# Gated delta recurrence: keys' norms through ScalarE's Ln and Exp, one PSUM reader in the convolution, and the first latent columns handed out ahead of the third pair's output

## The chip, the cores and the metric

The kernel runs on one core of a Trainium2 chip. The metric is device time in microseconds (us) of one launch; several executions of a kernel give a median. Engines are written as in the profile: PE (TensorE), DVE (VectorE), ACT (ScalarE), POOL (GpSimd) and SP (SyncE, which issues DMAs).

## What is computed

The reference is a mixer block followed by a second block; all the work of the change lies in the second. There, `h` (512 rows, 1024 wide) and a context `hc` (256 rows) are projected by one wide matrix `w_in`. Its columns give queries, keys and values of eight heads, an output gate `z`, and, further on, the latents of an attention branch (MLA, 704 columns). The part that matters, cut down:

```
def _centred_conv(x, w):                      # five taps along the rows
    return sum(xp[:, i:i + t] * w[i] for i in range(k_w))

def _l2norm(x):
    return x * lax.rsqrt(jnp.sum(x * x, axis=-1, keepdims=True) + EPS)

def _gdn_inputs(qkv, beta_logit, decay_logit, conv_w, a_log, dt_bias):
    qkv = jax.nn.silu(_centred_conv(qkv, conv_w))
    q, k, v = jnp.split(qkv, ...)
    q = _l2norm(q); k = _l2norm(k)
    ...

def _chunk_gated_delta(q, k, v, g, beta, state0):
    a_mat = jnp.where(strict, einsum('bhnid,bhnjd->bhnij', kb, k) * decay, 0.0)
    t_mat = lax.linalg.triangular_solve(eye + a_mat, eye, lower=True, unit_diagonal=True)
    ...
    s_final, o = lax.scan(step, state0, ...)  # states, chunk after chunk

def _gdn_out(o, z, w_norm):
    return _rms(o, w_norm) * jax.nn.silu(z)
...
q, kv = latents @ ...                         # the MLA branch, from cq, ckv, k_rope
```

The recurrence runs in both directions of the rows, in float32; the kernel makes each float32 product from three products of split halves (hi with hi, lo with hi, hi with lo).

## The kernel before

`gdn` takes the eight heads in four pairs, 0 to 3. For a pair, in the order in which the program is written:

- `inputs`: `feat` projects the keys. For each of two column tiles, `mm3s` (L234, L235, L237: 24 matmuls) fills a PSUM bank `pg` from 512 rows of `h`, 128x512 each, and another from the 256 rows of `hc`, 128x256 each. There are two `pg` banks. `conv` takes a bank out by ACT twice: L1254 copies it to `raw` in SBUF, L1255 copies it scaled by the middle tap to `acc`; DVE adds the four other taps (L1261), ACT applies Silu (L1263, with a table load where the last function was another). `turn` transposes on PE and evicts (L1293, L1296), ACT squares with a row sum `kss` (L1316). POOL adds 1e-6 (L1319, `kn`), raises to -1/2 (L1321) and multiplies (L1322, `krt`, the norm's root). Then the queries, in the same way.
- `values`: the same for the values, whose eviction L1296 is scaled by the root.
- `betas`: ACT's logarithm of `kn` (L1351, one per head) and DVE's reciprocal (L1353).
- `within`: Gram products on PE (L1375, L1377) and the decays' sums with a mask (L1384, L1385), exponentials on ACT (L1387), products on DVE (L1389 to L1391), and the triangular matrices gathered into `inv` by ACT (L1395) and DVE (L1397).
- `states`: the inversion on DVE. L1405 transposes, then 31 columns are eliminated by pairs of a product L1413 and a subtraction L1416 (122 instructions), then two transposes L1418 and L1419. PE's 32x32 products L1433 take the result of L1418 first and that of L1419 after; further small products and six state steps (L1490 to L1534) follow.
- `output`: two products for `z` (Silu, L1550), norms, a transpose on PE (L1565), a product with `z` on DVE (L1567), and a DMA out (L1568).

The driver writes `states` of pair p, then all of `inputs` to `within` of pair p+1, then `output` of pair p. Behind `states` of the last pair comes `tail`: `mla_latent`, the latents in three blocks of columns (256, 256, 192; 24 matmuls for each of three outputs of a block, evicted at L987), and a gate's products; then `output(3)`. A scheduler sets the order on PE, ACT, DVE and POOL from that written order as priority: whatever of later code is ready fills the places where a chain waits. Each engine then runs its own queue strictly in order. So PE projects the next pair during the state steps and during DVE's inversion; "fill" below is such work.

Weights come in groups of four blocks of 128 rows through six shared slots (`wp`, tag `w`): `wraw` by SP's DMA, `whi` by ACT (L178), `wlo` by DVE (L179). Those of queries, keys and values were split earlier (`parts`) and come as `whi` and `wlo` directly; those of `z` and of the latents are split on the spot.

## Time and profile before

| | us |
|---|---|
| three runs | 2277.0, 2276.74, 2273.09 |
| their median | 2276.74 |
| profiled execution, its own time | 2269.84 |
| its span in the trace | 2268.0 |
| PE busy / DVE / ACT / POOL in the span | 96% / 52% / 45% / 11% |
| mean granted clock of TensorE | 0.986 |

The recurrence takes the stretch from about 900 to 1500 us. The trace counts PE's matmuls with pipelined, modelled ends, so that a row's duration is longer than the spacing of starts; the spacing is what a matmul costs. A clock of 1.00 is 2.4 GHz and one of 0.5 is 1.2 GHz. In a timeline row the first number is the start, the second the time of the whole row, and the bracket at its end the idle time of that engine just before it, with what ended it.

### The profile page before, as it was taken

The page shows a single profiled execution, that of the slowest core. Times are in us where ns is not written, and L with a number is a line of the kernel's source. Part 1 is how long each engine was busy: PE and PEld are TensorE (multiplying, and loading weights), DVE is VectorE, ACT ScalarE, POOL GpSimd, SP SyncE. Part 2 cuts the span into 40 slices and gives each one's busy share as a digit, 9 for nine tenths or more (in the row PEclk, how much of TensorE's full clock was granted, in tenths as well). Part 3 has the DMA queues.
Part 4 walks back from the last instruction along what each step waited for, and adds up shares of the span by engine and source line. Part 5 has one row for each costly group of instructions (what it writes and reads, how often), then busy time and mean ns, then how long its engine had stood idle before and what let it go on. Part 6 is the DMA issues. An engine that isn't in the chain of part 4 may idle for free. (4 is left out here: it accounts for less than half of the span.)

```text
span 2268.0 us, 38197 instructions
## 1 busy us (share of the span) xinstructions
PE 2166.3 (96%) x15367; PEld 1921.6 (85%) x15367; DVE 1186.8 (52%) x2636; ACT 1019.6 (45%) x2072; POOL 257.4 (11%) x411
## 2 busy tenths in 40 slices
PE   7999999999999999988999998999999998999999
PEld 7889988788889889867787888789998797898988
DVE  3654453656443233658687775337775444434343
ACT  4542243545443232666666664446564224314231
POOL 0221000001000001203121211201110011020102
PEclk9999999999999999999999998999999999999999
DMA  5233476555772332521222110331013442323232
GB/s 171 74 132 122 159 262 212 173 189 187 248 254 88 98 107 89 183 75 53 75 67 89 53 61 13 97 116 37 30 38 110 169 140 73 99 90 102 94 93 103
DMA packets 195816, 262.05 MB, mean 116 GB/s; under 512 B 12343, under 2 KB 157495, under 8 KB 195639
## 3 DMA queue, kind: packets, MB, share of 16 engines
q1 hardware_dynamic: 188864, 244.61, 33.3%
q10 hardware_dynamic: 6775, 15.00, 1.8%
q8 instruction: 121, 1.98, 0.3%
q14 instruction: 56, 0.46, 0.1%
HBM read 223.39 MB, written 36.18 MB: 114 GB/s over the span
## 5 line engine op out<-in xcount | busy, mean ns | idle before, releaser
L179 DVE TENSOR_TENSOR wlo<-wraw,whi 128x1024 fp32r<-128x1024 f32 (+2 forms) x267 | 321.7, 1205 | 413.6 <-PE pg L235 204.8
L178 ACT ACTIVATE whi<-wraw 128x1024 fp32r<-128x1024 f32 (+2 forms) x267 | 277.0, 1037 | 445.1 <-DMA wraw<-in_w_mlp_out 104.5
L234 PE MATMUL pg<-xhi,whi 128*128 128x512 f32 (+1 forms) x1104 | 428.8, 391 | 25.3 <-ACT a L1255 15.9
L235 PE MATMUL pg<-xlo,whi 128*128 128x512 f32 (+1 forms) x1104 | 425.0, 387 | 0.0
L237 PE MATMUL pg<-xhi,wlo 128*128 128x512 f32 (+1 forms) x1104 | 293.5, 385 | 2.3 <-DVE wlo L179 2.3
L234 PEld LDWEIGHTS pg<-xhi,whi 128*128 128x128 f32 x1104 | 210.6, 191 | 72.5 <-ACT a L1255 18.1
L235 PEld LDWEIGHTS pg<-xlo,whi 128*128 128x128 f32 x1104 | 210.5, 191 | 37.0
L237 PEld LDWEIGHTS pg<-xhi,wlo 128*128 128x128 f32 x1104 | 202.9, 190 | 41.3 <-DVE wlo L179 3.0
L234 PE MATMUL pg<-whi,xhi 128*128 128x256 f32 (+1 forms) x608 | 160.3, 293 | 3.5 <-ACT whi L178 2.6
L235 PE MATMUL pg<-whi,xlo 128*128 128x256 f32 (+1 forms) x608 | 156.5, 288 | 0.0
L234 PE MATMUL sc<-whi,a 128*128 128x256 f32 x560 | 138.2, 281 | 1.6 <-ACT whi L178 1.6
L234 PE MATMUL pg<-whi,a 128*128 128x256 f32 x560 | 138.1, 281 | 0.5 <-DVE a L148 0.5
L235 PE MATMUL sc<-whi,a 128*128 128x256 f32 x560 | 138.4, 281 | 0.0
L235 PE MATMUL pg<-whi,a 128*128 128x256 f32 x560 | 138.0, 280 | 0.0
L234 PEld LDWEIGHTS pg<-whi,xhi 128*128 128x128 f32 x608 | 118.2, 194 | 10.6 <-ACT whi L178 5.2
L235 PEld LDWEIGHTS pg<-whi,xlo 128*128 128x128 f32 x608 | 117.9, 194 | 0.7 <-issue 0.4
L1261 DVE SCALAR_TENSOR_TENSOR a<-a,convw,a 128x511 f32<-128x511 f32 (+3 forms) x160 | 98.2, 642 | 20.1 <-ACT a L1255 19.2
L234 PEld LDWEIGHTS sc<-whi,a 128*128 128x128 f32 x560 | 105.6, 189 | 2.0 <-ACT whi L178 1.8
L237 PE MATMUL pg<-wlo,xhi 128*128 128x256 f32 (+1 forms) x608 | 101.5, 288 | 5.7 <-DVE wlo L179 5.7
L936 POOL TENSOR_TENSOR a<-a,a 128x256 f32<-128x256 f32 x64 | 48.8, 763 | 511.2 <-DVE a L935 510.5
L234 PEld LDWEIGHTS pg<-whi,a 128*128 128x128 f32 x560 | 105.6, 189 | 0.9 <-DVE a L148 0.9
L235 PEld LDWEIGHTS sc<-whi,a 128*128 128x128 f32 x560 | 106.0, 189 | 0.2
(477 smaller groups left out, 4543.1 us busy)
## 6 DMA issues: line engine op xcount, KB each, us to landing
wraw<-in_w_in SPq DMA_DIRECT2D x56, 512.0 KB
fraw<-in_w_mod SPq DMA_DIRECT2D x48, 512.0 KB
parts<-fraw SPq DMA_DIRECT2D x48, 512.0 KB
wraw<-in_w_gate_up SPq DMA_DIRECT2D x44, 512.0 KB
wraw<-in_w_mlp_in SPq DMA_DIRECT2D x32, 512.0 KB
wraw<-in_w_mlp_out SPq DMA_DIRECT2D x32, 512.0 KB
whi<-parts SPq DMA_DIRECT2D x26, 512.0 KB
wlo<-parts SPq DMA_DIRECT2D x26, 512.0 KB
```

The source lines that it names most:

```text
L178: nc.scalar.activation(hi, raw, AF.Copy)
L179: self.wlo_eng.tensor_tensor(lo, raw, hi.bitcast(F32), op=OP.subtract)
L234: mm(out, A[k][0], B[k][0], start=start and k == 0, stop=False)
L235: mm(out, A[k][late], B[k][1 - late], start=False, stop=False)
L237: mm(out, A[k][1 - late], B[k][late], start=False, stop=stop and k == n - 1)
L936: nc.gpsimd.tensor_tensor(self.x[t][:, cs], self.x[t][:, cs], u, op=OP.add)
L1261: dve.scalar_tensor_tensor(y, v, wi, y, op0=OP.mult, op1=OP.add)
```

## The change

Three functions change, in four ways.

1. In `conv` the scaled copy reads `raw`, the first copy's result in SBUF, in place of the PSUM bank.
2. The roots of the keys' norms move from POOL to ACT: a logarithm of `kss` plus 1e-6 and an exponential of half of it, once for both heads of a pair. POOL's three instructions per head go. `betas` reuses the logarithm, and DVE makes the reciprocals of both heads with two instructions.
3. `mla_latent` becomes a generator that stops once behind its first block of columns, and `tail` becomes the generator `beside`. The driver advances it once behind `within(3)` and ahead of `output(2)`, and once more behind `states(3)`.
4. SP's order follows: the two weight loads of `z` of pair 2 come behind the loads of the first block of latents.

In instructions POOL goes from 416 to 393, and ACT (1920), DVE (2638), PE (13837) and SP (526) keep their counts. ACT's table loads stay 49 in all: per pair 11, 11, 8 and 8 before, and 11, 10, 10 and 7 now.

```
--- before.py
+++ after.py
@@ -866,11 +866,12 @@
         def away(j):
             return lambda i, p: nc.scalar.dma_start(GD[j, i], p)
 
-        def tail():
-            self.latent = self.mla_latent(H, HC, w)
+        def beside():
+            yield from self.mla_latent(H, HC, w)
             gates(0, range(4), away(0))
-
-        OD = self.gdn(H, HC, w, tail)
+            yield
+
+        OD = self.gdn(H, HC, w, beside())
         self.wlo_eng = nc.vector
         self.psum(**BANKS_C)
         self.phase(**PHASE_C)
@@ -969,6 +970,7 @@
 
     def mla_latent(self, H, HC, w):
 
+
         nc, ap = self.nc, self.ap
         act, dve = nc.scalar.activation, nc.vector
         con = self.hb
@@ -985,6 +987,8 @@
                 for t2, ps in self.proj_tok(X, None, 0, n, fn, W):
                     for i in range(2):
                         act(Z[o + 2 * t2 + i][:, f0:f0 + fn], ps[:, i], AF.Copy)
+            if f0 == 0:
+                yield
         kr = con.tile([128, 6, 64], F32, name="kr")
         ssr = con.tile([128, 6], F32, name="ssr")
         CQ = [con.tile([128, 2, 512], F32R, name="cq", tag=f"inv{k}") for k in range(3)]
@@ -1019,7 +1023,7 @@
         for i in range(2):
             nc.scalar.dma_start(gq[64 * i:64 * i + 64], bass.AP(tensor=nm.tensor, offset=nm.offset + 128, ap=[[1, 64], [1, 1]]))
         nc.gpsimd.tensor_scalar(ropq, ropq, gq, None, op0=OP.mult)
-        return [[c[:, 0], c[:, 1]] for c in CQ], CKV, kr, ssr, ropq, gq
+        self.latent = [[c[:, 0], c[:, 1]] for c in CQ], CKV, kr, ssr, ropq, gq
 
     def mla(self, first, CQ, CKV, kr, ssr, ropq, gqr):
 
@@ -1236,7 +1240,7 @@
         g["rows"] = rg
         yield g
 
-    def gdn(self, H, HC, w, tail):
+    def gdn(self, H, HC, w, beside):
         nc, ap = self.nc, self.ap
         mm, act, dve = nc.tensor.matmul, nc.scalar.activation, nc.vector
         con = self.const
@@ -1245,6 +1249,9 @@
         tm = [con.tile([128, 136], F32, name=f"invt{v}") for v in range(2)]
         nc.gpsimd.memset(X, 0.0)
 
+        eps = con.tile([128, 1], F32, name="keps")
+        nc.gpsimd.memset(eps, 1e-6)
+
         def conv(ps, tile):
 
             raw, acc = (self.page([sum(p.shape[1] for p in ps)]) for _ in range(2))
@@ -1252,7 +1259,7 @@
             for p in reversed(ps):
                 n = p.shape[1]
                 act(raw[:, o:o + n], p, AF.Copy)
-                act(acc[:, o:o + n], p, AF.Copy, scale=cw[:, 48 + tile:49 + tile])
+                act(acc[:, o:o + n], raw[:, o:o + n], AF.Copy, scale=cw[:, 48 + tile:49 + tile])
                 for i in (0, 1, 3, 4):
                     wi = cw[:, 24 * i + tile:24 * i + tile + 1]
                     a, b = max(0, 2 - i), min(n, n + 2 - i)
@@ -1307,21 +1314,18 @@
                 fv = None, ahead(2048)[1]
                 fk = ahead(1024)
             kc = [conv(ps, 8 + h0 + f) for f, ps in enumerate(feat(1024 + pair * 256, True, fk))]
-            n2, root = [], []
+            ss = self.hb.tile([128, 2, 6], F32, name="kss", bufs=2)
             for f, (c, raw) in enumerate(kc):
                 kt = self.page([6, 128])
                 turn(c, kt)
-                ss = self.tmp.tile([128, 6], F32, name="kss")
                 for t in range(6):
-                    act(raw[:, t * 128:t * 128 + 128], kt[:, t], AF.Square, accum_out=ss[:, t:t + 1])
-                n2.append(self.hb.tile([128, 6], F32, name=f"kn2{f}", bufs=2))
-                root.append(self.hb.tile([128, 6], F32, name=f"krt{f}", bufs=2))
-                nc.gpsimd.tensor_scalar(n2[f], ss, 1e-6, None, op0=OP.add)
-                r = self.hb.tile([128, 6], F32, name="krs", bufs=2)
-                nc.gpsimd.tensor_tensor(r, n2[f], self.mhalf[:, :6], op=OP.pow)
-                nc.gpsimd.tensor_tensor(root[f], r, n2[f], op=OP.mult)
+                    act(raw[:, t * 128:t * 128 + 128], kt[:, t], AF.Square, accum_out=ss[:, f, t:t + 1])
                 kT.append(c.rearrange("p (a b) -> p a b", a=6))
                 ktok.append(kt)
+            ln = self.hb.tile([128, 2, 6], F32, name="kln", bufs=2)
+            act(ln, ss, AF.Ln, bias=eps)
+            root = self.hb.tile([128, 2, 6], F32, name="krt", bufs=2)
+            act(root, ln, AF.Exp, scale=0.5)
             qc = [conv(ps, h0 + f) for f, ps in enumerate(feat(pair * 256, False))]
             for q, sq in qc:
                 qT.append(q)
@@ -1332,7 +1336,7 @@
                 s1 = self.tmp.tile([128, 4], F32, name="qss")
                 dve.tensor_copy(s1, pq)
                 sq_.append(self.rstd(s1, 1.0 / 128, 128e-6, "qrs"))
-            return (qT, kT, ktok), (root, sq_), n2, fv
+            return (qT, kT, ktok), (root, sq_), (ss, ln), fv
 
         def values(pair, root, fv):
 
@@ -1340,20 +1344,20 @@
             for f, ps in enumerate(feat(2048 + pair * 256, True, fv)):
                 c, _ = conv(ps, 16 + 2 * pair + f)
                 vt = self.page([6, 128])
-                turn(c, vt, root[f])
+                turn(c, vt, root[:, f])
                 vtok.append(vt)
             return vtok
 
         def betas(pair, n2):
             h0, nb, bd = 2 * pair, [], []
+            ss, ln = n2
+            inv = self.hb.tile([128, 2, 6], F32, name="kin", bufs=2)
+            dve.tensor_scalar(inv, ss, 1e-6, None, op0=OP.add)
+            dve.reciprocal(inv, inv)
             for f in range(2):
-                ln = self.hb.tile([128, 6], F32, name="kln", bufs=2)
-                act(ln, n2[f], AF.Ln)
-                inv = self.hb.tile([128, 6], F32, name="kin", bufs=2)
-                dve.reciprocal(inv, n2[f])
                 for out, nm, v, op in ((nb, "nb", ln, OP.subtract), (bd, "bd", inv, OP.mult)):
                     out.append(self.hb.tile([128, 6, 2], F32, name=f"k{nm}{f}", bufs=2))
-                    dve.tensor_tensor(out[f], g[nm][:, :, h0 + f::8], v[:, :, None].to_broadcast([128, 6, 2]), op=op)
+                    dve.tensor_tensor(out[f], g[nm][:, :, h0 + f::8], v[:, f, :, None].to_broadcast([128, 6, 2]), op=op)
             return nb, bd
 
         D2 = range(2)
@@ -1584,8 +1588,8 @@
                 vtok = values(pair + 1, rest[0], fv)
                 nb, bd = betas(pair + 1, n2)
                 EM = within(pair + 1, *keys[:2], nb)
-            else:
-                tail()
+            if pair > 1:
+                next(beside)
             output(pair, O, sq_)
         return OD
```

Lines of the changed program are four higher than those of before from `inputs` to `states` (L1405 is L1409, L1418 is L1422, L1567 is L1571).

DVE around the start of the inversion of pair 3, the last, before. `w_...` are matrices of `within(3)`, `a_14126` and `a_14153` the two gates `z` of pair 2:

```order
L1389 TENSOR_TENSOR w_14059<-w_14045,sc 128x256
L1389 TENSOR_TENSOR w_14081<-w_14067,sc 128x256
L179 TENSOR_TENSOR wlo<-wraw,whi 128x1024
L1390 TENSOR_TENSOR w_14059<-w_14046,sc 128x512
L1567 SCALAR_TENSOR_TENSOR a_14126<-pt,onw,a_14126 128x512
L1391 TENSOR_TENSOR w_14046<-w_14046,sc 128x512
L1390 TENSOR_TENSOR w_14081<-w_14068,sc 128x512
L1567 SCALAR_TENSOR_TENSOR a_14153<-pt,onw,a_14153 128x512
L1391 TENSOR_TENSOR w_14068<-w_14068,sc 128x512
L1397 STREAM_TRANSPOSE inv<-w_14081 32x192 x4
L1405 STREAM_TRANSPOSE inv<-inv 128x1024
L179 TENSOR_TENSOR wlo<-wraw,whi 128x1024
```

The same place now, from the last products of `within(3)`:

```order
L1394 TENSOR_TENSOR w_14005<-w_13992,sc 128x512
L1395 TENSOR_TENSOR w_13992<-w_13992,sc 128x512
L1394 TENSOR_TENSOR w_14027<-w_14014,sc 128x512
L1395 TENSOR_TENSOR w_14014<-w_14014,sc 128x512
L1401 STREAM_TRANSPOSE inv<-w_14027 32x192 x4
L1409 STREAM_TRANSPOSE inv<-inv 128x1024
L1417 TENSOR_TENSOR invt_9499<-inv 128x31
L179 TENSOR_TENSOR wlo<-wraw,whi 128x1024
L1420 TENSOR_TENSOR inv<-inv,invt_9499 128x31
```

Inside the inversion DVE now also has, behind 30 of its 122 instructions, a second `wlo`, and, behind 69, the two products with the gate:

```order
L1417 TENSOR_TENSOR invt_9500<-inv 128x126
L1420 TENSOR_TENSOR inv<-inv,invt_9499 128x14x9
L1571 SCALAR_TENSOR_TENSOR a_14247<-pt,onw,a_14247 128x512
L1571 SCALAR_TENSOR_TENSOR a_14274<-pt,onw,a_14274 128x512
L1420 TENSOR_TENSOR inv<-inv,invt_9500 128x14x9
L1417 TENSOR_TENSOR invt_9499<-inv 128x130
```

The two L1567 have moved from ahead of the inversion into it, and it holds three `wlo` (behind 1, 30 and 115 of its instructions) where it held two.

ACT among the exponentials of `within(2)`, before; `a_12796` and `a_12823` are the gates `z` of pair 1:

```order
L1387 ACTIVATE w_12658<-pt,knb_12633 128x128 x2
L1387 ACTIVATE w_12680<-pt,knb_12633 128x128 x2
L1387 ACTIVATE w_12715<-pt,knb_12641 128x128
L1395 ACTIVATE inv<-w_12672 32x192 x4
L1387 ACTIVATE w_12715<-pt,knb_12641 128x128
L1387 ACTIVATE w_12737<-pt,knb_12641 128x128 x2
L1387 ACTIVATE w_12716<-sc,knb_12641 128x128 x4
L1387 ACTIVATE w_12738<-sc,knb_12641 128x128 x3
L1395 ACTIVATE inv<-w_12729 32x192 x4
L1387 ACTIVATE w_12738<-sc,knb_12641 128x128
L1550 ACT_TABLE_LOAD
L1550 ACTIVATE a_12823<-pg 128x512
```

and now:

```order
L1391 ACTIVATE w_12675<-pt,knb_12601 128x128 x2
L1391 ACTIVATE w_12697<-pt,knb_12601 128x128 x2
L1554 ACT_TABLE_LOAD
L1554 ACTIVATE a_12756<-pg 128x512
L1391 ACT_TABLE_LOAD
L1391 ACTIVATE w_12676<-sc,knb_12601 128x128 x4
L1391 ACTIVATE w_12698<-sc,knb_12601 128x128 x4
L1399 ACTIVATE inv<-w_12689 32x192 x4
L1554 ACT_TABLE_LOAD
L1554 ACTIVATE a_12783<-pg 128x512
```

The Silu of the first gate (with its table) has moved in among the exponentials, and a table load of L1391 stands behind it.

PE at the last mask product of `within(3)` (L1384 and L1385), before; `whi,xhi` in this order are products of the latents, `xhi,wlo` those of `z`:

```order
L237 MATMUL pg_14128<-xhi_9304,wlo_14098 128x512 x3
L1384 MATMUL sc_14074<-rg_10074,sel16_7300 128x512
L1385 LDWEIGHTS idb_7306
L1385 MATMUL sc_14074<-gmask_7310,idb_7306 128x512
L237 MATMUL pg_14128<-xhi_9304,wlo_14098 128x512
L1565 MATMUL pt_14174<-ident_83,w2048_13237 128x128 x4
L1565 MATMUL pt_14200<-ident_83,w2048_13238 128x128 x4
L234 MATMUL pg_14857<-whi_14847,xhi_9304 128x256
L235 MATMUL pg_14857<-whi_14847,xlo_9305 128x256
```

and now:

```order
L1388 MATMUL sc_14020<-rg_10067,sel16_7300 128x512
L1389 LDWEIGHTS idb_7306
L1389 MATMUL sc_14020<-gmask_7310,idb_7306 128x512
L234 MATMUL pg_14108<-whi_14047,xhi_9304 128x256
L235 MATMUL pg_14108<-whi_14047,xlo_9305 128x256
L237 MATMUL pg_14108<-wlo_14048,xhi_9304 128x256 x4
L234 MATMUL pg_14108<-whi_14053,xhi_9304 128x256
L235 MATMUL pg_14108<-whi_14053,xlo_9305 128x256
```

and, 66 products of the latents further on, the last of 48 products of `z`:

```order
L235 MATMUL pg_14249<-xlo_9305,whi_14218 128x512
L237 MATMUL pg_14249<-xhi_9304,wlo_14219 128x512 x4
L1569 MATMUL pt_14295<-ident_83,w2048_13197 128x128 x4
L1569 MATMUL pt_14321<-ident_83,w2048_13198 128x128 x4
L234 MATMUL pg_14968<-whi_14958,xhi_9304 128x256
L235 MATMUL pg_14968<-whi_14958,xlo_9305 128x256
```

Products of the first block of latents have taken the place of `z` ahead of the last mask product, and all 48 products of `z` (128x512) with the transposes L1569 (L1565 before) now stand behind it and behind the rest of that block.

## Rows read from the trace of the kernel before

**Rows 1.** Stretches: length, busy us by engine, granted clock, DMA share, GB/s.

```profile
1048.75:1116.60 67.85, 63.70 (x710) 54.58 (x710) 44.17 (x109) 55.61 (x152) 15.67 (x25) 0.97 0.13 40
1116.60:1150.20 33.60, 29.82 (x158) 25.05 (x157) 32.25 (x141) 10.29 (x25) 0.04 (x1) 1.00 0.42 139
1150.20:1226.60 76.40, 74.32 (x771) 63.31 (x772) 52.37 (x122) 62.10 (x178) 19.21 (x32) 0.98 0.17 50
1226.60:1259.75 33.15, 28.27 (x150) 23.88 (x149) 32.08 (x141) 9.60 (x21) 0.01 (x1) 1.00 0.41 134
1259.75:1335.90 76.15, 74.15 (x772) 63.81 (x773) 53.40 (x123) 63.38 (x179) 17.65 (x32) 0.98 0.10 31
1335.90:1368.60 32.70, 23.81 (x177) 22.66 (x175) 31.77 (x137) 9.59 (x20) 0.00 (x0) 0.91 0.21 64
```

**Rows 2.** Waits of PE, 900 to 1520 us: total, times, longest.

```profile
PE pg L234 <- ACT a L1255: 15.9, 8, 6.8
...
PE sc L1433 <- DVE inv L1418: 7.0, 3, 3.2
```

**Rows 3.** Timeline, pair 0's inversion: POOL, DVE and PE.

```profile
1026.03 11.16 POOL L1319 TENSOR_SCALAR kn<-kss 128x6 f32<-128x6 f32 x1 [52.54 <-ACT a L1316]
...
1046.07 2.04 DVE L1419 STREAM_TRANSPOSE inv<-inv 128x1024 f32<-128x1024 f32 x1
...
1048.75 0.44 PE L1433 MATMUL sc<-inv,w 32*32 32x32 f32 x28
```

**Rows 4.** Timeline of PE: starts of first L1433 products, pairs 2 and 3.

```profile
1259.75 0.28 PE L1433 MATMUL sc<-inv,w 32*32 32x32 f32 x4 [3.20 <-DVE inv L1418]
...
1368.63 0.39 PE L1433 MATMUL sc<-inv,w 32*32 32x32 f32 x4 [1.79 <-DVE inv L1418]
```

**Rows 5.** Timeline of PE: spacing of products, 512 and 256 wide, and 512 at half clock.

```profile
1328.84 0.39 PE L234 MATMUL pg<-xhi,whi 128*128 128x512 f32 x1
...
1329.76 0.39 PE L234 MATMUL pg<-xhi,whi 128*128 128x512 f32 x1
...
1359.34 0.28 PE L234 MATMUL pg<-whi,xhi 128*128 128x256 f32 x1
...
1360.05 0.28 PE L234 MATMUL pg<-whi,xhi 128*128 128x256 f32 x1
...
990.34 0.63 PE L235 MATMUL pg<-xlo,whi 128*128 128x512 f32 x1
...
990.76 0.63 PE L234 MATMUL pg<-xhi,whi 128*128 128x512 f32 x1
```

**Rows 6.** Timeline of DVE: where the inversions of pairs 1, 2 and 3 start.

```profile
1123.29 2.07 DVE L1405 STREAM_TRANSPOSE inv<-inv 128x1024 f32<-128x1024 f32 x1
...
1232.84 2.08 DVE L1405 STREAM_TRANSPOSE inv<-inv 128x1024 f32<-128x1024 f32 x1
...
1341.87 2.01 DVE L1405 STREAM_TRANSPOSE inv<-inv 128x1024 f32<-128x1024 f32 x1
```

**Rows 7.** Timeline of ACT and DVE around pair 3's inversion start.

```profile
1337.07 1.28 ACT L1550 ACT_TABLE_LOAD   x1
...
1338.99 0.75 DVE L1567 SCALAR_TENSOR_TENSOR a<-pt,onw,a 128x512 f32<-128x512 f32 x1 [0.47 <-ACT a L1550]
...
1343.81 1.18 DVE L179 TENSOR_TENSOR wlo<-wraw,whi 128x1024 fp32r<-128x1024 f32 x1
```

**Rows 8.** Timeline of SP, ACT and PE: a weight load inside pair 3's inversion.

```profile
1358.12 0.37 SPq L172 DMA_DIRECT2D wraw<-in_w_in  x1
...
1361.65 1.06 ACT L178 ACTIVATE whi<-wraw 128x1024 fp32r<-128x1024 f32 x1 [1.45 <-DMA wraw<-in_w_in]
...
1365.46 1.38 PE L237 MATMUL pg<-wlo,xhi 128*128 128x256 f32 x8 [3.99 <-DVE wlo L179]
```

**Rows 9.** ACT's groups by shape, 900 to 1540 us: copies from PSUM and from SBUF.

```profile
L1255 ACT ACTIVATE a<-pg,convw 128x512 f32<-128x512 f32 x24 | 16.7, 697 | 0.0
L1254 ACT ACTIVATE a<-pg 128x512 f32<-128x512 f32 x24 | 14.4, 601 | 35.5 <-PE pg L237 35.5
...
L147 ACT ACTIVATE a<-a 128x512 fp32r<-128x512 f32 x2 | 1.2, 622 | 0.0
```

More of the change, by code (lines that the diff above doesn't have):

```diff
@@ L1586, in gdn @@
                 EM = within(pair + 1, *keys[:2], nb)
-            else:
-                tail()
+            if pair > 1:
+                next(beside)
             output(pair, O, sq_)
```

46 lines of the change are left out of this document (24 added, 22 removed).

## Prediction, made before the changed kernel was run

> **What bounds the kernel now.** The table by stretches comes first [rows 1]. I cut it at two events of each pair: the end of the last mask product L1385 of `within`, and the start of the first L1433. Two kinds of stretch alternate. From L1433 to the end of the next `within` (67.85, 76.40, 76.15 us) PE is busy for 63.7, 74.3 and 74.2 us, with DVE and ACT well below: PE's own work sets the length. From there to the next L1433 (33.60, 33.15, 32.70 us) DVE is busy for 32.3, 32.1 and 31.8 us: the inversion sets the length, and PE only fills it. The list of PE's waits comes next [rows 2]. The largest is L1255, the second reader of a bank, with 15.9 us; the longest of its eight is 6.8 us. The timeline says what lies behind that one [rows 3]: POOL's L1319 took 11.16 us while DVE ran pair 0's inversion, ACT's logarithm waited for it, and L1254 and L1255 of the next queries stood behind that with both banks full. But it lies inside an inversion. L1419 ended at 1048.11, and PE began L1433 at 1048.75, only 0.64 us later. For pairs 2 and 3 PE still waited 3.20 and 1.79 us for L1418 [rows 4]. So most of the 15.9 us is idle time that would be idle a little later. What counts is how much of PE's work leaves the PE-bound stretches, and when each inversion starts and ends.
>
> **Prices.** Starts four products apart give 0.23 us for a 128x512 product (1328.84 to 1329.76), six apart 0.118 us for a 128x256 (1359.34 to 1360.05); at half clock a 128x512 costs 0.42 us [rows 5].
>
> **The change, part by part.**
>
> *One reader of the bank.* A bank comes free one copy (L1255, 0.70 us) earlier, so products start earlier inside the inversions and at pair 0's keys and values. Inside an inversion this is worth nothing. Ahead of pair 0's inversion one long wait for L1255 shortens by about 0.6 us, the overlapping rest of that copy. The copy from SBUF itself is dearer by some 0.02 us (622 against 601 ns, unscaled [rows 9]), 36 times, or 0.7 us on ACT, which is 0 on the path since ACT is not the bound in any stretch [rows 1]. The Trainium skill ("Perfetto Trace Analysis", Optimizing Scalar/DVE Operations) speaks against this edit: it gives ScalarE about 93 ns of access overhead for SBUF and 51 for PSUM. By its 42 ns the 36 copies would be an estimated 1.5 us of ACT in place of 0.7; the rows show about half of it, and either is covered.
>
> *Roots on ACT.* POOL's 24 instructions go, and with them the 11.16 us. Pair 0 gains at most the 0.64 us at L1433. In return PE, its fill done early, stands idle for some 8 us ahead of L1433 (the 6.8 us moved to the end, and a short wait or two), and the clock may be low behind that: 0 at least, and at most 2.0 us, as much again as the 3% that the first stretch already lost (0.03 x 67.85); taken 0.5, since pair 3's waits already show such a start. Six more 128x512 products now stand ahead of the last mask product of `within(0)`, 1.4 us, half of it taken as hidden: 0.7. Pair 0 together: -0.64 - 0.6 + 0.5 + 0.7, or 0.0. The table loads stay 49, at 1.28 us each [rows 7], but shift: pair 2's `within` gets two more (L1554's in the midst of the exponentials and L1391's behind it). Their bounds are 0 and 2.6 us at the start of that inversion. Pair 1 has that order already, and its inversion starts 6.7 us behind the last mask product (1123.29 - 1116.6), pair 2's 6.2 us (1232.84 - 1226.6) [rows 1, 6]; I take the difference, 0.4. The Trainium skill ("ScalarE: Activation LUTs", Table sets: the hidden batching unit) has one set hold both ln and exp, so that a logarithm followed by an exponential needs one load; the built order has a load ahead of each. By that page's section on the cost of the load, 2.66 us for a switch, the two loads would be an estimated 5.3 us at most; the row has 1.28 for one.
>
> *The latents' first block ahead of `output(2)`.* Counted in the built order, the 128x512 products between L1433 of pair 1 and the end of `within(2)` fall from 98 to 83 (15 x 0.23 = 3.4 us); ahead of `within(3)` 99 become 44, and 78 of 128x256 come in (55 x 0.23 - 78 x 0.118 = 3.4 us). Ahead of `within(1)` two are added (0.5). The work reappears inside the inversions of pairs 2 and 3, where PE has room: 33.15 - 28.27 and 32.70 - 23.81 us idle [rows 1]. It doesn't count in full, since state steps leave PE small holes that products filled. The first and second PE-bound stretches differ by 32 products of 128x512 and 24 of 128x256, 10.2 us, and by 8.55 us in length: 0.84 for one. So pair 1 +0.4; pair 2 -2.9; pair 3 -2.9.
>
> *What pair 3's inversion pays.* The two L1567 (0.75 us each [rows 7]) no longer stand ahead of it but inside it, with a third `wlo` (1.18 us). Ahead, little is gained: `within(3)` on ACT now has four copies L1399 (1.5 us) between its last exponentials, so I put L1409 5.6 us behind the last mask product, against 6.0 before (1341.87 - 1335.9). Inside, 1.5 + 1.2 = 2.7 more. Net +2.3, and L1437 comes about 35 us behind the mask product instead of 32.7. Now the rest of the chain. PE ends the block's 66 products at +7.8 (66 x 0.118), the first 22 of `z` at +12.9, and then wants `wlo` of the second half of `z`'s weights. Their slot is free at about +6.5; a load issued at 1358.12 let ACT begin at 1361.65 [rows 8], so 3.5 us on, at +10, ACT makes `whi` until +11.1. DVE comes to that `wlo` behind 30 of 122 instructions (0.166 us each: 26.8 us less two transposes and two `wlo`, over 122), at +13.8, done at +15.0. PE waits 2.1 us, does 26 more (6.0) and the transposes (1.0), +22.0. DVE comes to the L1571 at +21.5. So half a microsecond more, if the clock stays up; taken 0.7. Pair 3: -2.9 + 2.3 + 0.7, or +0.1.
>
> **The sum.** 0.0 + 0.4 + (-2.9 + 0.4) + 0.1 = -2.0 us. On the profiled execution (2269.84, of which the span is 2268.0) that is 2267.8; it ran 6.9 us below the median of the runs. Against the median, 2276.74 - 2.0 = 2274.7.
>
> **Rivals.**
>
> *The gain stays.* The fill counts in full (-3.4 for pairs 2 and 3 each), and the inversion of pair 3 starts earlier by the two L1567 and their waits (1.5 + 0.7) and gives only that back: +0.5 in place of +3.0. Pair 0's six products are hidden in full, -0.6 in place of 0.0. Then -0.6 + 0.5 - 3.0 - 2.9, or -6.0: 2270.7. For it: PE busy throughout the stretches, DVE's room in them. Against: the stretches' ratio 0.84, and the copies between the exponentials.
>
> *Slower: pair 3's `z` at half clock.* Its place is the wait for the second `wlo` of `z`. If that wait of 2.1 us brings the clock down, as waits around 1344 and 1361 us in the same inversion do (mean clock 0.91 in that stretch [rows 1]; 3.99 us in one wait [rows 8]), the 26 products take 26 x 0.19 = 4.9 us more, the 24 latents' products behind them 2.8, DVE stands at L1571 with half its inversion undone, and the state steps of pair 3 start that much later. From the point where PE reaches the transposes behind +21.5, every microsecond is one on the path. With 7.7 us in place of 0.7 the sum is +5.0: 2281.7.
>
> *The change doesn't show.* Banks free earlier, roots earlier, all inside inversions whose end is DVE's: the fill is reordered but PE-bound stretches don't shrink, since the products that left are replaced by holes of the state steps. Then about 0 to +1: 2277. It lies inside the forecast's own class.
>
> **How the numbers follow.** About 0.2% of the time, 4.5 us, is what a measurement can tell from no change. The forecast with the last rival (-4.5 to +4.5) has 0.47; the gain that stays, past -4.5, 0.33; slower, past +4.5, 0.20. The range leaves out the ends of both: below, -8.7 (the gain with the banks' waits at pair 0 in full); above, the slower rival's +5. So 2268 to 2281.7; the forecast's own part of it is 2272.2 to 2281.2.
>
> **What would show it.** In the trace of the changed kernel: no 11 us instruction on POOL and no 6.8 us wait for L1261 or L1262; instead waits for L1422 at L1437 of some 8 us for pair 0. PE-bound stretches near 68.2, 73.9 and 73.3 us. Pair 2's inversion starting 6.6 us, pair 3's 5.6 us behind the last mask product, and pair 3's L1437 35 us behind it. A wait of PE for a `wlo` of about 2 us in pair 3's fill, and DVE reaching the L1571 with less than 1 us of waiting. If pair 3's stretch stays at 32.7 us, the gain stays; if DVE waits there for several microseconds at a clock of 0.5, the slower rival holds. The forecast is wrong, too, if PE-bound stretches shrink by much more or less than 0.84 of the products that leave them.

## The result: slower by 17 us, and the profile after

| | us |
|---|---|
| changed kernel, median of 7 runs | 2294.14 (2284.04 to 2297.01) |
| kernel before, median of 7 runs | 2276.74 (2271.49 to 2278.84) |
| ratio, with its 95% interval | 1.0075 (1.0061 to 1.0089) |
| profiled execution after, its own time and span | 2295.04, 2293.2 |
| mean granted clock after (before 0.986) | 0.978 |

The forecast was 2274.7 us, 2 us faster, with a range up to 2281.7. The time lies outside it.

The table by stretches of the kernel after, cut at the events of [rows 1] (end of the last mask product, first block product L1437), with the start ahead and the end behind; columns as in [rows 1]:

```profile
946.58:1025.67 79.09, 72.59 (x363) 57.01 (x364) 38.02 (x88) 53.41 (x126) 6.03 (x12) 0.94 0.28 85
1025.67:1061.54 35.87, 26.91 (x145) 22.91 (x145) 35.45 (x148) 13.29 (x36) 0.01 (x1) 0.93 0.32 103
1061.54:1134.52 72.98, 67.09 (x711) 57.27 (x712) 46.27 (x111) 58.09 (x160) 14.74 (x26) 0.92 0.12 38
1134.52:1167.65 33.13, 30.68 (x162) 26.07 (x162) 32.27 (x141) 11.54 (x25) 0.01 (x1) 1.00 0.49 159
1167.65:1240.25 72.60, 71.75 (x756) 61.61 (x757) 51.69 (x121) 63.47 (x176) 14.91 (x26) 0.95 0.12 38
1240.25:1274.09 33.84, 30.94 (x164) 26.27 (x163) 32.29 (x141) 11.78 (x26) 0.01 (x1) 1.00 0.47 154
1274.09:1352.02 77.93, 73.59 (x796) 66.46 (x797) 52.56 (x122) 61.33 (x177) 13.57 (x26) 0.91 0.07 20
1352.02:1386.86 34.84, 24.20 (x147) 21.02 (x146) 32.73 (x138) 8.38 (x18) 0.01 (x1) 0.87 0.24 74
1386.86:1515.69 128.83, 121.19 (x1057) 108.62 (x1058) 51.32 (x104) 61.98 (x160) 21.05 (x39) 0.96 0.23 70
```

And the three stretches of the kernel before that [rows 1] leaves out: the start (from pair 0's first projection of 512 columns), pair 0's inversion, the end:

```profile
935.56:1010.21 74.65, 69.39 (x357) 54.21 (x358) 37.18 (x88) 52.20 (x126) 10.47 (x18) 0.95 0.30 90
1010.21:1048.75 38.54, 30.68 (x151) 25.29 (x149) 38.47 (x150) 16.50 (x44) 14.68 (x8) 0.91 0.29 96
1368.60:1497.44 128.84, 121.57 (x1057) 108.77 (x1057) 51.27 (x104) 61.06 (x159) 21.96 (x39) 0.96 0.24 70
```

| stretch | before | forecast | after |
|---|---|---|---|
| start | 74.65 | 74.8 | 79.09 |
| inversion of pair 0 | 38.54 | 37.9 | 35.87 |
| L1437 of pair 0 to `within(1)` | 67.85 | 68.2, and 0.5 for the clock | 72.98 |
| inversion of pair 1 | 33.60 | 33.6 | 33.13 |
| L1437 of pair 1 to `within(2)` | 76.40 | 73.9, with 0.4 for the inversion's start | 72.60 |
| inversion of pair 2 | 33.15 | 33.2 | 33.84 |
| L1437 of pair 2 to `within(3)` | 76.15 | 73.3 | 77.93 |
| inversion of pair 3 | 32.70 | 35.0 | 34.84 |
| end | 128.84 | 129.5 | 128.83 |

The recurrence, the only place that I had costed, is 7.2 us longer in these two profiles. The other 18 us between them (25.2 in all) lie ahead of it (11.0: the first projection starts at 946.58 and not 935.56) and behind it, where no instruction of the change stands. Some of that is the luck of the profiled runs: the one of before ran 6.9 us below its median, the one of after 0.9 above.

### The profile page after: what moved, and what is told of

The parts are those of the page before. It is cut to its first block, busy times and chain, and to the rows that moved or that the text cites. A ratio compares the mean times of both kernels' runs of the same rounds, so it can differ in the third digit from the quotient of the medians.

```text
span 2293.2 us, 38170 instructions
## 1 busy us (share of the span) xinstructions
PE 2183.3 (95%) x15367; PEld 1940.2 (85%) x15367; DVE 1186.5 (52%) x2636; ACT 1021.6 (45%) x2072; POOL 227.1 (10%) x388
## 3 DMA queue, kind: packets, MB, share of 16 engines
q8 instruction: 121, 1.98, 0.4%
## 5 line engine op out<-in xcount | busy, mean ns | idle before, releaser
L237 PE MATMUL pg<-xhi,wlo 128*128 128x512 f32 (+1 forms) x1104 | 292.9, 385 | 4.3 <-DVE wlo L179 4.3
L237 PEld LDWEIGHTS pg<-xhi,wlo 128*128 128x128 f32 x1104 | 202.5, 190 | 43.6 <-DVE wlo L179 5.3
L234 PE MATMUL sc<-whi,a 128*128 128x256 f32 x560 | 141.2, 284 | 1.6 <-ACT whi L178 1.6
L234 PE MATMUL pg<-whi,a 128*128 128x256 f32 x560 | 140.9, 283 | 0.5 <-DVE a L148 0.5
L235 PE MATMUL sc<-whi,a 128*128 128x256 f32 x560 | 141.2, 284 | 0.0
L235 PE MATMUL pg<-whi,a 128*128 128x256 f32 x560 | 140.8, 283 | 0.0
L237 PE MATMUL pg<-wlo,xhi 128*128 128x256 f32 (+1 forms) x608 | 103.3, 291 | 9.0 <-DVE wlo L179 9.0
L234 PEld LDWEIGHTS pg<-whi,a 128*128 128x128 f32 x560 | 107.6, 192 | 1.0 <-DVE a L148 0.9
L235 PEld LDWEIGHTS pg<-whi,a 128*128 128x128 f32 x560 | 107.5, 192 | 0.0
L1268 DVE SCALAR_TENSOR_TENSOR a<-a,convw,a 128x511 f32<-128x511 f32 (+3 forms) x160 | 98.2, 643 | 15.9 <-ACT a L1262 14.8
```

The costliest lines, as they stand in the source:

```text
L234: mm(out, A[k][0], B[k][0], start=start and k == 0, stop=False)
L235: mm(out, A[k][late], B[k][1 - late], start=False, stop=False)
L237: mm(out, A[k][1 - late], B[k][late], start=False, stop=stop and k == n - 1)
L1268: dve.scalar_tensor_tensor(y, v, wi, y, op0=OP.mult, op1=OP.add)
```

## Experiments

Ratios are to the kernel before, measured beside each batch of kernels, and have 95% intervals. Differences in us are to that batch's own median of the kernel before (2273.6 to 2274.45).

### Where code is slower that the change doesn't touch

Ahead of 900 us both kernels issue the same instructions in the same order, but for the memset of `keps`, and yet the distance between them grows. Products of 128x256 show it. Timeline of PE, before and after, in the second half: first products of groups of four L237, each group 12 products behind the last (rows between left out).

```profile
2003.27 0.63 PE L237 MATMUL sc<-wlo,a 128*128 128x256 f32 x4
...
2030.13 0.64 PE L237 MATMUL sc<-wlo,a 128*128 128x256 f32 x4
```

```profile
2003.15 0.64 PE L237 MATMUL sc<-wlo,a 128*128 128x256 f32 x4
...
2030.51 0.64 PE L237 MATMUL pg<-wlo,a 128*128 128x256 f32 x4
```

19 groups, 228 products: 26.86 us before and 27.36 after, 0.1178 and 0.1200 us for one, at a granted clock of 1.00 in both. What differs is where tiles lie. In each of these products one operand is moving (128x256, here the weights) and one is held (128x128, loaded by an LDWEIGHTS, here activations in a page). The diff allocates `kss` in another pool and adds `keps`. In the built programs the weights' slots begin at byte 25472 of a partition and the pages at 89024 before, at 25504 and 88992 after: the distance is 63552 bytes in one and 63488 in the other, a multiple of 128. My first idea was another, that the slots had lost a 64-byte alignment.

Before, with a dead tile of 4 bytes (a slot of 32) or 64 bytes in the constants, which moves slots and pages together (the first; the second has [128, 16]):

```
+        eps = con.tile([128, 1], F32, name="keps")
+        nc.gpsimd.memset(eps, 1e-6)
```

> The kernel before, with one dead constant of 128x1 float32 (32 bytes per partition) that is only filled: every other instruction and its order are those of before, but all tiles of the pools behind it lie 32 bytes further, off the multiples of 64 on which they lay. Theory A (the 32-byte shift alone makes the 128x256 products dearer, 120 ns a start in place of 113 to 118, in the whole program): slower than before by 10 to 18 us, 2286 to 2294, and the offset grows from the first 700 us on, where the change touches nothing. Theory B (the loss of the changed kernel lies in the moved work of the recurrence, and the offsets elsewhere are chance of the clock): 0 +- 3 us.

> The same with a dead constant of 128x16 float32 (64 bytes): all tiles move by 64 bytes and stay on multiples of 64. Theory A: 0 +- 3 us against before. If it is the tile, its memset or any move of the layout that costs, and not the alignment: as slow as the one with 32 bytes.

The changed kernel with its `keps` widened, so that the slots are aligned as before:

```
-        eps = con.tile([128, 1], F32, name="keps")
+        eps = con.tile([128, 16], F32, name="keps")
...
-            act(ln, ss, AF.Ln, bias=eps)
+            act(ln, ss, AF.Ln, bias=eps[:, :1])
```

> The changed kernel with its constant eps made 64 bytes wide instead of 32; all engines' orders are the changed kernel's. Theory A with the prediction's sum for the moved work: 2.0 us faster than before, between -6 and +3, about 2275. Theory B: as slow as the changed kernel, +14 to +20 us.

Measured: 2273.93 (1.0001, 0.9989 to 1.0013), 2274.32 (1.0008, 0.9996 to 1.002) and, for the changed kernel, 2291.58 (1.008, 1.0064 to 1.0097). Alignment makes no difference that shows: theory A fell. What the first two keep and the third doesn't is the distance. So I changed that alone: a dead tile gives the changed kernel its 63552 bytes back (first diff), and `kss` of the kernel before, moved to the other pool, makes 63488 (second).

```
+        nc.gpsimd.memset(self.tmp.tile([128, 6], F32, name="kss0"), 0.0)
```

```
-                ss = self.tmp.tile([128, 6], F32, name="kss")
+                ss = self.hb.tile([128, 6], F32, name="kss", bufs=2)
```

> The changed kernel with one dead tile of 128x6 float32 in the pool of small temporaries, from which the change has taken kss away (64 bytes per partition, two buffers). All orders are the changed kernel's. It puts the pages, where the moving operands lie, back to their distance from the weights' slots: 63552 bytes from slot to first page as before, where the changed kernel has 63488, a multiple of 2048. Theory C (it is this distance that makes 128x256 products cost 120 ns in place of 113 to 118, in the whole program): faster than the changed kernel by 12 to 18 us; against before between -6 and +5, by the prediction's sum and the +5 that the third part alone showed. Theory B (the moved work): as slow as the changed kernel, +14 to +20.

> The kernel before with kss allocated in the pool of the recurrence instead of the small temporaries; no instruction or order changes, but the pages move to 63488 bytes from the weights' slots, as in the changed kernel. Theory C: slower than before by 8 to 15 us, with 128x256 products at 120 ns a start in the first block, where nothing of the change runs. Theory B: 0 +- 2 us.

Measured: the changed kernel falls to 2282.61 (1.0037, 1.0025 to 1.005), and the kernel before rises to 2282.91 (1.0038, 1.0022 to 1.0054), with every instruction in its old place. Timeline of PE, `before_hbkss`, the same products:

```profile
2004.14 0.64 PE L237 MATMUL pg<-wlo,a 128*128 128x256 f32 x4
...
2031.50 0.64 PE L237 MATMUL sc<-wlo,a 128*128 128x256 f32 x4
```

Again 27.36 us for 228 products. So 1.0038 of the 1.0075, 8.6 us, is the distance, and 1.0037, 8.4 us, is the change itself. `before_hbkss` came out as theory C had it (8 to 15). `after_tmp` did not: its text took the prediction's sum for the rest and allowed +5 over the kernel before, and +8.2 came. (It also calls the pages the place of the moving operands; in these products they have the held one.)

These products account for the whole of it. Summed over each trace, from each start of the 3360 products of 128x256 with a page to the start behind it, they take 398.9 us in the kernel before and 408.0 in `before_hbkss`, 409.8 in the changed kernel and 397.9 in `after_tmp`. And it is the distance, not the place of either operand: the pages of `after_pad64` begin at byte 89024, as in the kernel before, and it is slow; the slots of `before_pad32` begin at 25504, as in the changed kernel, and it is not. Two more kernels vary the distance: 63616 bytes, which is a multiple of 128 but not of 2048; and a shift of `xhi` and `xlo`, which had stood at a multiple of 128 from the slots in all kernels (the pages lie behind them and move along, to 63584).

```
+        nc.gpsimd.memset(self.tmp.tile([128, 8], F32, name="kss0"), 0.0)
```

```
+        self.nc.gpsimd.memset(self.xt.tile([128, 8], F32, name="xpad"), 0.0)
```

> The kernel before with a dead tile of 64 bytes more ahead of the pages: they move to 63616 bytes behind the weights' slots, 64 more than before, 128 more than in the changed kernel; no instruction changes but one memset. Theory C in its narrow form, the residue of the distance modulo 128 decides (0 is dear, 64 is cheap): 128x256 products with activations in pages start 120 ns apart again as in the changed kernel, and the time is 8 to 9 us above the kernel before, 2283 us. Rival, only residue 0 modulo 512 or more is dear: 117 ns as before, and 2274 us.

> The kernel before with a dead tile of 32 bytes between the weights' slots and xhi and xlo: these now stand 32 bytes off a multiple of 128 from the weights, the pages 96. Theory C: the 128x256 products with xhi and xlo as the held operand, most of them ahead of 450 us, start 118 instead of 119.7 ns apart, those with pages stay near 117.4; about 1600 x 1.5 ns, or 2.5 us less. The 128x512 products, whose moving operand is xhi or xlo, may go up from 227.3 towards 229.2 ns (seen for pages 64 bytes off): 0 to 5 us more. So 2272 to 2277 us, 2273 if the 512-wide ones stay. If the residue matters for pages alone, nothing changes: 2274.

`before_page128` takes 2284.87 (1.0042, 1.003 to 1.0055): the products are 0.1200 us apart again, so a multiple of 128 is enough to make them dear. `before_xt32` takes 2289.98 (1.0065, 1.0053 to 1.0077), and my expectation (2272 to 2277) fell: the 512-wide products pay far more than the 256-wide ones with `xhi` or `xlo` held gain (their median spacing ahead of 450 us goes from 0.120 to 0.117 us). Timeline of PE, kernel before and then `before_xt32`, the last L237 of 12 products each (all 512 wide; one line lower in the second):

```profile
651.47 1.07 PE L237 MATMUL pg<-xhi,wlo 128*128 128x512 f32 x4
...
670.51 1.07 PE L237 MATMUL pg<-xhi,wlo 128*128 128x512 f32 x4
```

```profile
671.19 1.10 PE L238 MATMUL pg<-xhi,wlo 128*128 128x512 f32 x4
...
679.59 1.10 PE L238 MATMUL pg<-xhi,wlo 128*128 128x512 f32 x4
```

19.04 us for 84 products before, 0.2267 each; 8.40 for 36, 0.2333 each; the clock is 1.00 in both. Why the distance matters no run shows.

### The three parts, alone and in pairs

All with the distance of the kernel before. Parts 1 and 2 without 3 were not run.

| parts | us | ratio |
|---|---|---|
| 1, one reader of the bank | 2274.43 | 0.9997 (0.9982 to 1.0012) |
| 2, roots on ACT | 2299.32 | 1.0109 (1.0087 to 1.0131) |
| 3, latents' block ahead | 2278.74 | 1.0024 (1.0013 to 1.0035) |
| 1 and 3 | 2270.75 | 0.9986 (0.9976 to 0.9997) |
| 2 and 3 | 2284.39 | 1.0036 (1.0023 to 1.0049) |
| all | 2282.61 | 1.0037 (1.0025 to 1.005) |

Each has its hunks of the diff and no others; where part 2 is in, the dead tile of `after_tmp` too. Their cores, parts 1, 2 and 3:

```
-                act(acc[:, o:o + n], p, AF.Copy, scale=cw[:, 48 + tile:49 + tile])
+                act(acc[:, o:o + n], raw[:, o:o + n], AF.Copy, scale=cw[:, 48 + tile:49 + tile])
```

```
-                nc.gpsimd.tensor_tensor(r, n2[f], self.mhalf[:, :6], op=OP.pow)
...
+            act(ln, ss, AF.Ln, bias=eps)
...
+            act(root, ln, AF.Exp, scale=0.5)
```

```
+            if f0 == 0:
+                yield
...
-            else:
-                tail()
+            if pair > 1:
+                next(beside)
```

> Only the first part, the convolution's scaled copy read from SBUF; layout as before. By the prediction: banks free earlier inside the inversions, worth 0 to 0.6 us, 36 copies dearer by 0.02 us off the path: 0 +- 1.5. If it is the copy's own price or its wait on the first copy that costs in the recurrence: +2 to +4.

> Only the third part, the latents' first block handed out ahead of pair 2's output; no new constant, layout as before. By the prediction's working (PE-bound stretch of pair 3 shorter by 2.9, its inversion later by 2.3 to 3): 0 +- 2 us. The rival in which pair 3's z runs at half clock behind the wait for its second wlo: +4 to +6. The rival in which the gain stays: -3.

> Only the second part, the roots on ScalarE, with the dead temporary tile that keeps the distance of pages and weights as before. By the prediction: POOL's 11 us wait goes, pair 0 gains at most 0.6, two more table loads in one pair cost 0.4 to 2.6: 0 +- 2. If the roots' order on ScalarE costs more than that: +3 or more.

> Parts 2 and 3 together (the roots on ACT, and the first block of latents handed out ahead of the third pair's output), the convolution as before, and the distance of weights and pages as before. Theory D, placement: what the roots alone cost (24.9 us) is mostly that the second wlo of the latents stands behind pair 3's inversion in DVE's queue, so that 119 products of 128x256 (14 us at 0.118) lose their place inside it; with the latents' block ahead of output(2), wlo stands behind 33 of the 122 instructions, those products are back, and the 13.6 us wait of PE is gone. Then 24.9 - 14 + 2 (two products with the gate and a third wlo inside the inversion) - 4 (fewer 128x512 products ahead of within(3)): about +9, or 2283 us (2280 to 2286). Rival, the parts add up: 24.9 + 5.4 = 30.3, or 2305 us. In the trace D expects pair 3's inversion stretch near 35 us with PE busy for 23 of it; the rival a wait for wlo above 10 us.

> Parts 1 and 3 together (one reader of the bank, and the first block of latents ahead of output(2)), the roots on POOL as before; no change in the layout. Theory D by stretches: the start up to the last mask product of within(0) +4.1, pair 0's inversion -2.6, the stretch behind it +4.6 (PE idle ahead of it and half clock behind), pair 1's inversion 0, the next stretch -2.5, then -0.7, pair 3's stretch -1.9 (55 products of 128x512 at the 0.272 us they cost among state steps, against 91 of 128x256 at 0.143), pair 3's inversion +2.4: +3.4, or 2278 us (2275 to 2281). If the parts simply add up: 0 + 5.4, or 2280 us. If the one reader is worth more once the latents fill pair 3, below 2274.

The parts don't add. Part 2 costs 24.9 us alone, 3 to 6 on top of part 3 (by the ratios and by the medians), and 11.6 on top of 1 and 3. What it costs alone shows in pair 3's inversion. DVE's `wlo` of the latents of that kernel there, and PE's wait:

```profile
1359.72 1.19 DVE L179 TENSOR_TENSOR wlo<-wraw,whi 128x1024 fp32r<-128x1024 f32 x1
1380.05 1.22 DVE L179 TENSOR_TENSOR wlo<-wraw,whi 128x1024 fp32r<-128x1024 f32 x1
```

```profile
1381.32 1.22 PE L237 MATMUL pg<-wlo,xhi 128*128 128x256 f32 x4 [13.63 <-DVE wlo L179]
```

Before, the first `wlo` of the block came ahead of the inversion:

```profile
1334.34 1.22 DVE L179 TENSOR_TENSOR wlo<-wraw,whi 128x1024 fp32r<-128x1024 f32 x1 [0.53 <-ACT whi L178]
```

and the second, that of the block's other half, right behind L1405 (1343.81, [rows 7]). With the roots alone each has slipped by one place: the first stands behind L1407 (L1405 before), the second behind 114 of the inversion's 122 instructions. PE waits for it for 13.6 us and is busy for 12.7 us of the inversion (23.8 before, [rows 1]); in the built order 52 products stand there and not 169, so some 14 us of latents' products come behind the inversion: the end takes 142.75 us where it took 128.84. The rest of the 24.9 lies in the stretches behind the inversions of pair 0 (73.39 us, 67.85 before; the clock, below) and of pair 1 (82.34, 76.40 before; why, stays open). With part 3, `z` is there to fill, and the second `wlo` comes early. The expectation for parts 2 and 3 (2283) held, and the sum of the two (2305) fell.

For 1 and 3 both sums fell: 2278 and 2280 expected, 2270.75 measured. The third case of that text, that one reader is worth more once the latents fill pair 3 (below 2274), has the number; that this is the cause is not shown. It is 3.5 us less than the kernel before, with an interval that just leaves out 1, and the only kernel here that beats both.

### What the roots cost on top of parts 1 and 3

The changed kernel, its distance mended, with the roots of pair 0 on POOL again, and the reverse, only those of pair 0 on ACT:

```
+            if pair == 0:
...
+                for f in range(2):
+                    nc.gpsimd.tensor_scalar(n2[:, f], ss[:, f], 1e-6, None, op0=OP.add)
+                    nc.gpsimd.tensor_tensor(r[:, f], n2[:, f], self.mhalf[:, :6], op=OP.pow)
+                    nc.gpsimd.tensor_tensor(root[:, f], r[:, f], n2[:, f], op=OP.mult)
+            else:
+                act(ln, ss, AF.Ln, bias=eps)
+                act(root, ln, AF.Exp, scale=0.5)
...
+            if pair == 0:
+                act(ln, ss, AF.Ln, bias=eps)
```

The last two lines stand in `betas`. The second kernel has `pair > 0` in both places.

> The changed kernel with the distance of weights and pages as before, and with the roots of pair 0's keys on POOL again (its logarithm late, in betas); pairs 1 to 3 have them on ACT. Theory E: of what the roots cost, most lies in the start, up to the last mask product of within(0). There ACT is busy throughout, and the logarithm and the exponential of pair 0, with a Silu between them and a table load ahead of each of the three (1.28 us each), stand ahead of the copies that free the queries' bank: PE waits 0.70 and 0.93 us, the clock falls behind that, and that stretch takes 87.5 us where it took 82.6 with the roots on POOL. So this kernel regains 4 to 5 us: 2278 us (2276 to 2280). Rival, the start's length is the six more products of 128x512 and the clock's chance: 2282 to 2283 as with all roots on ACT.

> The other half: pair 0's roots on ACT, those of pairs 1 to 3 on POOL; distance as before, all else as in the changed kernel. Theory E: the start stays at 87.5 us; behind it things stand as with the roots on POOL (the first stretch behind L1437 71.4 instead of 73.0, pair 3's 73.9 instead of 76.4): 2270.8 + 4.9, or 2276 us (2274 to 2279). Rival, the roots of the later pairs cost most, by the wait of 9 us ahead of L1437 and the half clock behind it: then this kernel is near 2271 to 2273, and the other near 2281.

`act0` takes 2276.59 (1.0014, 1.0001 to 1.0026), what theory E gave; `pool0` 2283.05 (1.0049, 1.003 to 1.0069), what its rival gave. The trace of `pool0` has its start 2.2 us shorter than the changed kernel with its distance mended (77.27 against 79.42), but its times don't show it; they spread over 14 us (2277.3 to 2291.7). So the roots of pairs 1 to 3 cost about 5 us with those of pair 0 on ACT (1.0037 against 1.0014). What those of pair 0 cost stays open: nothing by `pool0`, some 6 by `act0` against parts 1 and 3. That `act0` met theory E's number doesn't show E, which wanted `pool0` 4 to 5 us lower.

## Why the prediction was wrong, step by step

The two largest misses are a term that was not there at all (the layout, 8.6 us), and one that was mis-sized: the clock behind pair 0's L1437, put at 0.5 us, is about 4. The other steps follow in the order of the stretches.

**Left out: where tiles lie (8.6 us).** The prediction went through the order of instructions and through nothing else. That a small tile changes its pool stands in the diff, `self.tmp.tile` against `self.hb.tile`, and was taken for nothing. It is half of the result.

**"ACT is not the bound in any stretch": the table began too late.** [rows 1] begins at 1048.75. In the start ACT was full for a while before the change, and so was PE (columns as in [rows 1]; PE's 15.00, ACT's 14.86 of 15.00), so that more work on ACT has no room there:

```profile
950.00:965.00 15.00, 15.00 (x89) 12.06 (x88) 6.15 (x13) 14.86 (x36) 4.83 (x7) 1.00 0.42 138
```

Timeline of ACT after, there:

```profile
969.52 1.28 ACT L1326 ACT_TABLE_LOAD   x1
970.82 0.30 ACT L1326 ACTIVATE kln<-kss,keps 128x12 f32<-128x12 f32 x1
971.14 1.28 ACT L1270 ACT_TABLE_LOAD   x1
972.43 0.63 ACT L1270 ACTIVATE a<-a 128x512 f32<-128x512 f32 x1
973.08 1.28 ACT L1328 ACT_TABLE_LOAD   x1
974.38 0.21 ACT L1328 ACTIVATE krt<-kln 128x12 f32<-128x12 f32 x1
974.50 0.58 ACT L1261 ACTIVATE a<-pg 128x512 f32<-128x512 f32 x1
```

The exponential and its load stand ahead of the copy that frees the queries' bank, and PE waits there and at a square a little later:

```profile
975.13 0.42 PE L223 MATMUL pg<-xhi,whi 128*32 128x512 f32 x1 [0.69 <-ACT a L1261]
983.49 1.05 PE L1335 MATMUL pt<-ones,a 128*128 128x1 f32 x8 [0.94 <-ACT a L1332]
```

The start was forecast at +0.1 us (0.7 for six products, 0.6 gained at the bank) and is +4.4: six products (1.4), idle time of PE 6.5 us where it was 5.26 (1.2), and the rest partly the clock. The roots have a small part in that: with those of pair 0 on POOL (`pool0`) the wait of 0.69 us is gone and that of 0.94 still there, and the roots alone make the start 75.64 us, 1.0 more than before. Most of it comes with part 1, which brings the six products: alone it has 79.12, roots on POOL. How much of that is the clock show part 1 alone and parts 1 and 3, whose orders are the same up to here:

```profile
939.89:1019.01 79.12, 73.11 (x363) 57.72 (x364) 37.85 (x88) 50.78 (x124) 9.53 (x18) 0.94 0.29 85
```

```profile
936.87:1012.96 76.09, 70.09 (x363) 54.90 (x364) 37.82 (x88) 50.73 (x124) 9.52 (x18) 0.98 0.30 88
```

3 us apart, at mean clocks of 0.94 and 0.98: so much of the start's 4.4 is not safe from a single profile. Length times clock is 74.4 and 74.6 for the two, 74.3 for the changed kernel and 70.9 before: some 3.5 us of the start's growth is not the clock. Six products and idle time are 2.6 of that; the rest stays open.

The Trainium skill ("ScalarE: Activation LUTs", Table sets: the hidden batching unit) would have a logarithm followed by an exponential need one load. The rows don't agree: in pair 1 only copies stand between the two, and the exponential has its load all the same, so for these programs the rows decide (timeline of ACT after).

```profile
1079.20 1.28 ACT L1326 ACT_TABLE_LOAD   x1
1080.49 0.30 ACT L1326 ACTIVATE kln<-kss,keps 128x12 f32<-128x12 f32 x1
1080.70 1.26 ACT L1530 ACTIVATE w<-w,g_gl 128x128 f32<-128x128 f32 x4
1081.97 1.28 ACT L1328 ACT_TABLE_LOAD   x1
1083.27 0.21 ACT L1328 ACTIVATE krt<-kln 128x12 f32<-128x12 f32 x1
```

**Pair 0's inversion: the gain was under-read.** Forecast 0.64 us, measured 2.67. I took the distance from the end of L1419 to L1433; the first products need L1418 alone, which ended at 1046.20, 2.55 us ahead of 1048.75. After, L1437 starts 0.15 us behind L1422. Timeline of DVE, before:

```profile
1043.99 2.21 DVE L1418 STREAM_TRANSPOSE inv<-inv 128x1024 f32<-128x1024 f32 x1
```

**The idle time ahead of L1437: the clock term was mis-sized.** This is the step of the recurrence that failed most. I foresaw the wait (8 us; it is 8.96) and gave the clock behind it 0.5 us, 2.0 at most. Timeline of PE after:

```profile
1061.54 0.39 PE L1437 MATMUL sc<-inv,w 32*32 32x32 f32 x4 [8.96 <-DVE inv L1422]
```

Waits of PE after, 900 to 1540 us (total, times, longest):

```profile
PE sc L1437 <- DVE inv L1422: 15.2, 4, 9.0
...
PE pg L234 <- ACT a L1261: 3.2, 1, 3.2
```

The first 12.25 us behind L1437 or L1433: before, with part 1 alone (which has the same products up to `within(1)` as before, 66 of them 512 wide), and after:

```profile
1048.75:1061.00 12.25, 10.80 (x357) 9.55 (x357) 9.24 (x21) 11.83 (x31) 3.95 (x10) 0.86 0.02 5
```

```profile
1054.93:1067.20 12.27, 10.23 (x330) 9.11 (x332) 10.33 (x20) 11.75 (x29) 6.00 (x14) 0.58 0.02 4
```

```profile
1061.54:1073.80 12.26, 10.26 (x346) 9.25 (x346) 10.10 (x17) 11.85 (x31) 6.03 (x14) 0.64 0.02 5
```

The granted clock is 0.86 where PE came to L1433 from its fill, and near 0.6 where it had waited. The low clock had been there before the change, too, but in another place. The 6.8 us wait of [rows 2] ended at 1038.54, and the clock stood at 0.5 inside the inversion, where DVE was busy throughout; now it stands there behind L1437 (columns as in [rows 1], before and after):

```profile
1035.30:1042.10 6.80, 3.56 (x8) 2.81 (x9) 6.80 (x41) 3.28 (x6) 3.48 (x3) 0.50 0.01 3
```

```profile
1061.50:1070.30 8.80, 6.76 (x281) 6.33 (x283) 7.64 (x14) 8.53 (x24) 5.54 (x12) 0.50 0.02 5
```

The whole stretch up to the mask product takes 67.8 to 69.4 us in the seven kernels in which PE doesn't wait there (the one before, its five variants, and part 3 alone with 69.44), and 71.4 to 75.8 in the nine of part 1 or 2 in which it does. Part 1 alone, with no product added, has 72.43 at a mean clock of 0.91 (0.97 before): the clock's share is 72.43 x 0.09 less 67.85 x 0.03, 4.5 us, which is the whole difference. For the changed kernel the same sum (72.98 x 0.08 less 67.85 x 0.03) gives 3.8 of 5.1. So the waits at the banks that parts 1 and 2 take away (3.2 us are left of 15.9, [rows 2]) come back at the end, in the changed kernel as one wait, in front of PE-bound work, and the clock behind it takes more than the inversion gained. The length of that last wait doesn't set the price: with part 1 alone it is 2.08 us, behind one of 4.13, and pairs 1 and 2 of the kernel before have 1.98 and 3.20 us there with a clock of 0.86 behind.

**Pair 2: right.** Forecast -2.9 and +0.4, measured -3.8 and +0.7. Its inversion starts 6.89 us behind the last mask product (6.6 forecast).

**Pair 3's fill: the products went, the time didn't.** Forecast -2.9, measured +1.8. In this stretch a product stands among state steps and costs more than back to back: 0.272 us for 512 columns before (27.2 us of starts for 100), 0.145 for 256 after part 3 alone (13.2 for 91). So the exchange of 55 for 78 is worth 55 x 0.272 - 78 x 0.145, 3.7 us. Against that PE is idle for 4.3 us (2.0 before), and the clock is 0.91 (0.98). With part 3 alone, where 47 go and 89 come in (12.8 and 12.9 us), the stretch is as long as before (76.38 against 76.15), its inversion 2.4 us longer, and the kernel slower. The step that failed is that the stretch's waits and its clock were taken as they were before; that the products' term holds is worked out here and not shown. Nor is +1.8 safe: the changed kernel, `after_tmp`, `after_pad64` and `pool0` have the same products there and take 77.93, 76.36, 75.85 and 75.52 us, at mean clocks of 0.91, 0.93, 0.95 and 0.98. None comes near 73.3.

**Pair 3's inversion: right.** +2.1 (2.3 forecast), and the end unchanged (0.7 forecast). DVE after, inside it:

```profile
1357.61 2.06 DVE L1409 STREAM_TRANSPOSE inv<-inv 128x1024 f32<-128x1024 f32 x1
1359.82 1.22 DVE L179 TENSOR_TENSOR wlo<-wraw,whi 128x1024 fp32r<-128x1024 f32 x1
1365.10 1.22 DVE L179 TENSOR_TENSOR wlo<-wraw,whi 128x1024 fp32r<-128x1024 f32 x1
1373.83 1.40 DVE L1571 SCALAR_TENSOR_TENSOR a<-pt,onw,a 128x512 f32<-128x512 f32 x2
1382.66 1.22 DVE L179 TENSOR_TENSOR wlo<-wraw,whi 128x1024 fp32r<-128x1024 f32 x1
1384.66 2.06 DVE L1422 STREAM_TRANSPOSE inv<-inv 128x1024 f32<-128x1024 f32 x1
```

L1409 starts 5.6 us behind the mask product and L1437 34.8 (5.6 and 35 forecast); DVE comes to L1571 21.8 us behind it (21.5) and doesn't wait. PE's longest wait in there, 8.58 us, is for the third `wlo`; the prediction doesn't name it, and the end is no longer for it.

**The rivals.** "The gain stays" and "the change doesn't show" fell. The slower one gave the right sign by the wrong mechanism: PE's wait for the second `wlo` is 0.94 us and not 2.1, and DVE doesn't wait at L1571. The time of part 3 alone (4.9 us by medians, 5.4 by the ratio) is the rival's +5.0, but its trace places only 2.6 of it where part 3 changes anything (0.2 and 2.4 above). Another 1.1 and 1.6 lie in pair 0's inversion (39.64) and the stretch behind it, where its order is that of before; kernels with that order differ nearly as much there between themselves (38.3 to 39.3 and 67.8 to 69.3). PE's wait for the second `wlo` is 1.08 us there, so the rival's mechanism isn't seen in it either.

**One reader of the bank.** The copy from SBUF costs 725 ns where the scaled one from PSUM cost 697 [rows 9], 28 ns more; the Trainium skill ("Perfetto Trace Analysis", Optimizing Scalar/DVE Operations) gives about 93 and 51 ns for the two accesses, 42 apart. The direction agrees, the measured 28 decides, and nothing on the path hangs on it: part 1 alone is 0.9997.

## What to carry to other kernels

Read the diff for allocations too: a small tile that changes its pool moves every later tile, and here that cost as much as all moved work. Idle time taken from the middle of an inversion that another engine bounds isn't gone but can come back at its end, and what matters is what PE does next, and at which clock. Test a change's parts alone and in pairs: the part that costs 25 us alone costs 3 to 6 beside another, and the two other parts together beat both kernels.
